# Release order kept, the last pair's weights by blocks in turn, row sums through TensorE, and a reordered start and routing end

## The chip, the cores and the metric

The kernel runs on one core of a Trainium2 chip. The metric is the device time of one execution in microseconds (us). Engines are named as the profile names them: PE is TensorE's matmul (PEld its weight load), DVE is VectorE, ACT is ScalarE, POOL is GpSimd, and SP is SyncE, whose queue issues most DMA transfers.

## The reference, cut to what matters

One encoder layer on 512 tokens of width 1024 in float32: an embedding layer norm, two attentions (A windowed with a sink, B latent) that read one projection `w_in`, their output projection, a layer norm, a mixture of 32 experts (each token goes to one group of 8 and to two experts in it), and a last layer norm.

```python
    h = layer_norm(x, ln_emb_g, ln_emb_b)
    proj = h @ w_in[l]
    ...
    h = layer_norm(DEEPNORM_ALPHA * h + mixed, ln_attn_g[l], ln_attn_b[l])
    ffn = hierarchical_moe(h, w_group[l], b_group[l], w_expert[l], b_expert[l], w_gate[l], w_up[l], w_down[l])
    h = layer_norm(DEEPNORM_ALPHA * h + ffn, ln_ffn_g[l], ln_ffn_b[l])
```

## The kernel before, in words

Tokens stand in four tiles of 128 (`xs[t]` as loaded, `z[t]` the residual stream), and the width of 1024 in two halves of 512. Products up to the routing are made in three passes on a split operand: `hth`/`htl` are the high and low part of the transposed, normed tokens, `wh`/`wl` those of a weight chunk `wf`. `split` makes the high part with a copy on ScalarE and the low part with a subtraction on another engine.

**The start.** The loop over `t` calls `layer_norm` (L203 and L204, two halves each: subtract the mean and multiply by the gain `lng`, then scale and add `lnb`), transposes the tile with the identity `ident`, which is a part of the constants `cst`, and splits the transposed values. The gain and the bias are loaded as 128 copies of a row, in four transfers on SP ahead of `cst`. For the first weight chunk POOL makes the low parts (L209). The first token tile's products begin with the high weights.

**The heads.** In two halves `c` of the heads, `heads` transposes and splits the queries of each token tile. Attention B's first units are scheduled beside the last of them.

**The routing's end.** The layer norm after attention is applied for tile 0, then 1, then `a` and `b` (tiles 2 and 3). `route(t)` picks a tile's experts in a chain of small DVE operations, `add_z` adds the output projection to `z`, `norm_gain`, `norm_bias`, `gain` and `shift` apply the norm, and `gather(t, ...)` collects the first two experts' tokens by products with a selection matrix into `gk`, which becomes `xT0`.

**The expert loop.** The experts are worked in 16 pairs. For a pair, `gates` (L1243) multiplies 64 gathered tokens of each of the two experts by `w_gu`, over 8 blocks `j` of the width, the two experts' products side by side in TensorE's columns; `gated` makes `hid`; `down` (L1263) multiplies by `w_dn`; `put` (L1276) weighs the result, adds the scaled residual of the gathered row, and `scatter` (L1269) writes the rows to `moe_rows` in HBM. Weights sit in a ring of six slots, and a pair's weights are asked for three pairs ahead, on SP, in `load_next` and `load_next_dn`: an issue waits until the products that read the old contents are done. In slots 0 and 1 the first half of `w_gu` is made of two pieces of 512 KB, so that they come free after two blocks each. Pair 0 runs two blocks of its gates, then the products `places` (L1368), which tell which rows the next pairs need, then the other six.

**The tail.** The last pair isn't scattered. `weighted` leaves its rows split in `y2`, and `pz_part` (L1310) multiplies them by `sT`, the transposed selection of their tokens, into `pz` in PSUM. The rows of the other pairs come back from `moe_rows` as `rows0` and `rows1`, two for each token. `rows_add` (L1480) adds the two, `total` (L1503) adds `pz` and sums the row, `square` (L1509) sums the squares, `factor` makes the reciprocal root, and `scale`, `gain`, `bias` or `gain_first` and `scale_bias` (L1529, L1534) end the norm. The order on every engine is the written one here.

## Time and profile before

| | |
|---|---|
| median of three runs | 594.92 us (592.09 to 598.53) |
| the profiled execution | 591.33 us, its span 589.5 us |
| granted TensorE clock, mean | 0.970 of full speed |
| PE busy | 523.4 us (89%) |
| DVE busy | 322.6 us (55%) |
| ACT busy | 222.1 us (38%) |
| POOL busy | 99.9 us (17%) |
| read from HBM | 133.14 MB |

The span runs from the first to the last instruction of the profiled execution. Busy shares are means over stages that differ: up to about 327 us the products of the attentions and their projections, then the 16 pairs, and from 545 us the last pair and the final norm.

### The profile page before, as it was taken

The numbers are of one execution on the slowest core, as the hardware profiler recorded it, in microseconds if no ns is written. First come the engines' busy times: TensorE is split into PE (matmuls) and PEld (weight loads), VectorE is DVE, ScalarE is ACT, GpSimd is POOL, SyncE is SP. The second block draws the span as 40 slices with busy tenths as digits, with TensorE's granted clock in tenths as the row PEclk, the third lists the DMA queues.
The fourth block names the chain that finished last, engine by engine and source line by source line (L and its number), as shares of the span: only waits on it lengthen the run. The fifth ranks groups of instructions, "written<-read, shape, count | busy, mean of one in ns | idle before, by whom it ended". The sixth has DMA issues, their size and how long they took to land. (4 is left out here: it accounts for less than half of the span.)

```text
span 589.5 us, 8004 instructions
## 1 busy us (share of the span) xinstructions
PE 523.4 (89%) x2756; PEld 331.8 (56%) x2757; DVE 322.6 (55%) x882; ACT 222.1 (38%) x477; POOL 99.9 (17%) x141
## 2 busy tenths in 40 slices
...
GB/s 279 280 290 81 102 43 0 59 81 42 85 16 58 1 1 212 289 367 39 66 258 259 280 391 410 420 415 415 411 417 400 421 418 391 412 420 416 264 267 142
DMA packets 46268, 141.76 MB, mean 240 GB/s; under 512 B 12380, under 2 KB 19420, under 8 KB 37009
## 3 DMA queue, kind: packets, MB, share of 16 engines
...
q10 hardware_dynamic: 1152, 2.10, 0.9%
...
HBM read 133.14 MB, written 16.25 MB: 253 GB/s over the span
## 5 line engine op out<-in xcount | busy, mean ns | idle before, releaser
L1243 PE MATMUL p_gu<-w_gu,xT 128*64 128x512 f32 x512 | 125.0, 613 | 15.0 <-DMA w_gu<-in_w_gu 14.1
L1243 PEld LDWEIGHTS p_gu<-w_gu,xT 128*64 128x64 f32 x512 | 39.6, 141 | 95.6 <-issue 70.0
L1247 ACT ACTIVATE hid<-p_gu 128x256 f32<-128x256 f32 x16 | 6.1, 384 | 176.0 <-PE p_gu L1243 163.9
L1248 DVE TENSOR_TENSOR hid<-hid,p_gu 128x256 f32<-128x256 f32 x16 | 6.7, 421 | 113.9 <-ACT hid L1247 113.8
L1263 PE MATMUL p_y<-w_dn,hidT 128*64 128x512 f32 x256 | 59.9, 611 | 1.0 <-issue 0.6
L1276 DVE SCALAR_TENSOR_TENSOR xg<-p_y,wsl,xg 128x512 f32<-128x512 f32 x30 | 22.5, 751 | 28.4 <-PE p_y L1263 26.5
L1263 PEld LDWEIGHTS p_y<-w_dn,hidT 128*64 128x64 f32 x256 | 17.5, 140 | 31.4 <-issue 29.3
L604 PE MATMUL ptr<-cst,pr 128*128 128x128 f32 x208 | 33.3, 278 | 1.9 <-ACT pr L562 1.4
L1034 POOL DMA_INDIRECT xg<-norm_rows,tok x16 | 16.5, 1032 | 104.5 <-PE p_y L1263 16.8
L1269 POOL DMA_INDIRECT moe_rows<-xg,idx x15 | 15.6, 1039 | 95.0 <-DVE xg L1276 69.6
L604 PEld LDWEIGHTS ptr<-cst,pr 128*128 128x128 f32 x208 | 24.9, 145 | 9.5 <-ACT pr L562 3.2
L577 ACT ACTIVATE pr<-pmm,bnm 128x512 f32<-128x512 f32 x32 | 22.0, 689 | 10.6 <-DVE bnm L574 9.7
L574 DVE TENSOR_REDUCE bnm<-pmm 128x1 f32<-128x512 f32 x32 | 21.9, 687 | 5.3 <-PE pmm L215 4.8
L215 PE MATMUL pmm<-wh,htl 128*128 128x512 f32 (+1 forms) x64 | 24.0, 374 | 0.0
L213 PE MATMUL pmm<-wh,hth 128*128 128x512 f32 (+1 forms) x64 | 23.8, 372 | 0.0
L214 PE MATMUL pmm<-wl,hth 128*128 128x512 f32 (+1 forms) x64 | 23.5, 368 | 0.0
L562 ACT ACTIVATE pr<-pr,rc 128x512 f32<-128x512 f32 (+2 forms) x32 | 20.6, 645 | 4.1 <-DVE rc L560 3.9
L590 DVE CUSTOM_DVE_ANT_0 sm<-pmm,mask,nsink 128x256 f32<-128x256 f32 (+1 forms) x32 | 17.4, 545 | 7.6 <-PE pmm L587 6.5
L215 PE MATMUL pwo<-wh,htl 128*128 128x512 f32 (+1 forms) x56 | 20.7, 370 | 0.0
L214 PE MATMUL pwo<-wl,hth 128*128 128x512 f32 (+1 forms) x56 | 20.5, 367 | 0.0
L213 PE MATMUL pwo<-wh,hth 128*128 128x512 f32 (+1 forms) x56 | 20.5, 367 | 0.0
L1232 ACT ACTIVATE xg<-xg,of 128x1024 f32<-128x1024 f32 x15 | 17.2, 1149 | 8.5 <-PE p_x L1228 7.8
...
## 6 DMA issues: line engine op xcount, KB each, us to landing
...
```

The costliest lines, as they stand in the source:

```text
L213: PE.matmul(ps, ah, bh, start=first, stop=False)
L214: PE.matmul(ps, ah, bl, start=False, stop=False)
L215: PE.matmul(ps, al, bh, start=False, stop=last)
L562: SC.mul(pr[:, :n], pr[:, :n], rc)
L574: V.tensor_reduce(nm, sp, AX.X, ALU.max, negate=True)
L577: exps_.append(SC.activation(pr[:, :S], sp, AF.Exp, bias=nm, accum_out=den).ins)
L590: V.tensor_tensor_reduce(sm[:, :nk], sp[:, :nk], mask[:, mo:mo + nk], 1.0, nsink[:, h:h + 1], ALU.add, ALU.min, nm)
L604: PE.transpose(pt[:, k * P:(k + 1) * P], pr[:, k * P:(k + 1) * P], ident)
L1232: SC.mul(pl["xg"], pl["xg"], pl["of"])
L1243: PE.matmul(pg[64 * i:64 * i + 64], xT[:, j, 64 * i:64 * i + 64], ws[i][0][j], start=(j == 0), stop=(j == 7))
L1263: r = PE.matmul(py[64 * i:64 * i + 64, :], hT[:, j, 64 * i:64 * i + 64], ws[i][1][n][:, j], start=(j == 0), stop=(j == 1))
L1276: V.scalar_tensor_tensor(y, py, pl["wsl"], y, ALU.mult, ALU.add)
```

## The change

- **Start.** `cst` and the gain and bias as columns (`geT`) are loaded first, on ACT's queue. ScalarE writes (x - mean) / deviation into `z`; gain and bias are applied to the transposed values, where they are one number to a partition, and `hf` holds the result in SBUF. The first chunk's low weights are made by DVE. The order of the first two token tiles is written by hand, and their products alternate. `z` itself gets gain and bias later, in 16 DVE operations of 128x512 after the `heads` of each tile, from `lgb`, which SP loads as 128 copies of a row when the second half of the heads begins.
- **Slots 0 and 1.** The half that consists of two pieces is the second half now.
- **Routing's end.** `norm_gain` and `norm_bias` of the second half of `a` come earlier; `route(a)` is cut after five steps and goes on behind `add_z(1)` and its statistics; `gather(a)` takes its second half first, and `shift(b, 1)` stands ahead of `gain(b, 0)`.
- **Pair 0.** Its blocks go in the order 4 to 7, 0 to 3. The four row fetches go in the order 1, 0, 2, 3, with `weights(1)` ahead of them. The work on the next pairs' columns and weights is moved behind `down`'s products, ahead of `put`.
- **Loads by blocks in turn.** Pair 3's and the last pair's `w_gu` are asked for block by block, one expert after the other, and the last pair's `w_dn` half by half.
- **Tail.** All `rows_add` are on DVE, the first tile's ahead of `weighted`'s `put`. `pz` starts with a product of the identity and the added rows. ScalarE takes the sum and the sum of squares of each half from PSUM, `gain_first` reads PSUM, and all four tiles end with `scale_bias`. The gain is multiplied by the root of 1024 ahead of time.

```diff
             return t
+        geT = cp.tile([P, 2, NK], F32, name="geT")
+        SC.dma_start(out=cst, in_=A["cst"][:, :C_KEEP])
+        SC.dma_start(out=geT, in_=A["ge_T"])
         load_x(0)
-        lg, lb = [lp.tile([P, D], F32, name=nm) for nm in ("lng", "lnb")]
-        for n in range(2):
-            for dst, nm in ((lg, "ln_emb_g"), (lb, "ln_emb_b")):
-                SY.dma_start(out=dst[:, 512 * n:512 * n + 512], in_=A[nm][512 * n:512 * n + 512].partition_broadcast(P))
-        SY.dma_start(out=cst, in_=A["cst"][:, :C_KEEP])
...
-                split(wf[:, :, :n], wh[:, :, :n], wl[:, :, :n], PO if nch[0] == 0 else V)
+                if nch[0]:
+                    split(wf[:, :, :n], wh[:, :, :n], wl[:, :, :n])
+                else:
+                    wfs.append(wf)
...
+        def scaled_x(t, kk):
+            rs, nb = nrm[t]
+            sl = slice(512 * kk, 512 * kk + 512)
+            SC.activation(z[t][:, sl], xs[t][:, sl], AF.Identity, scale=rs, bias=nb)
...
+                g_, b_ = [geT[:, i, 4 * kk + k:4 * kk + k + 1] for i in range(2)]
+                if eng is SC:
+                    SC.activation(hf[:, k], pt[:, k * P:(k + 1) * P], AF.Identity, scale=g_, bias=b_)
+                else:
+                    V.tensor_scalar(hf[:, k], pt[:, k * P:(k + 1) * P], g_, b_, ALU.mult, ALU.add)
...
+        with tc.manual_schedule(engines={V.engine, SC.engine, PE.engine, PO.engine}):
+            stats_half(0, 0)
+            stats_half(0, 1)
+            stats_end(0)
+            stats_shift(0)
             for kk in range(2):
-                pt = ptr()
-                for k in range(4):
-                    PE.transpose(pt[:, k * P:(k + 1) * P],
-                                 z[t][:, (4 * kk + k) * P:(4 * kk + k + 1) * P], ident)
-                pv = pt.rearrange("p (a b) -> p a b", a=4)
-                o = (slice(None), slice(4 * kk, 4 * kk + 4), slice(t * P, (t + 1) * P))
-                split(pv, hth[o], htl[o])
+                scaled_x(0, kk)
+                turn_x(0, kk)
+            gain_x(0, 0, range(4), V)
+            w_high(0)
+            stats_half(1, 0)
+            gain_x(0, 1, (1,), SC)
+            high(0, 0)
+            first_mm(0, hth, 0, 0)
+            low(0, 0)
...
-                heads(qt_, qth, qtl, c, t)
+                with tc.issue_after(heads(qt_, qth, qtl, c, t)):
+                    zt = z[t][:, 512 * c:512 * c + 512]
+                    V.tensor_tensor(zt, zt, lgb[0][:, c], ALU.mult)
+                    V.tensor_tensor(zt, zt, lgb[1][:, c], ALU.add)
...
-            if i == 0 and slot < 2:
-                return [(f"gu{slot}0{q}", 2 * q, 2) for q in range(2)]
+            if i == 1 and slot < 2:
+                return [(f"gu{slot}1{q}", 4 + 2 * q, 2) for q in range(2)]
...
+        def load_turns(e, slots, order):
+            ws = [{}, {}]
+            for h in order:
+                for ts in zip(*[gu_tiles(sl, h) for sl in slots]):
+                    for i in range(2):
+                        tag, j, n = ts[i]
+                        ws[i].update(zip(range(j, j + n), load_blocks(e + i, slots[i], tag, j, n)))
+            return [[w[j] for j in range(NK)] for w in ws]
...
-        place(a)
+        steps(ra)
+        place(1)
         sel0_(1)
-        sel0_(a)
         logits(b, 0)
         logits(b, 1)
         offset(b)
...
-        norm_gain(a, 1)
         biased(b)
-        norm_bias(a, 1)
         for i in range(2):
             keep(a, i)
         gather(0, range(2))
...
+        count(a)
         gather(1, range(2))
         steps(route(b))
+        place(a)
+        sel0_(a)
         count(b)
-        gather(a, [0])
         gain(b, 1, V)
+        gather(a, [1])
         place(b)
         sel0_(b)
-        gather(a, [1])
+        gather(a, [0])
+        shift(b, 1, V)
         gain(b, 0, V)
-        shift(b, 1, V)
...
+                pys.append(py)
+                if not between:
+                    put(slice(512 * n, 512 * n + 512), py)
+            if between:
+                between()
+                for n in range(2):
+                    put(slice(512 * n, 512 * n + 512), pys[n])
             return r.ins
...
+        def pz_rows(t, n, rows):
             tg = tags[t, n]
             pzs[t, n] = ps.tile([P, 512], F32, name="pz", tag=tg, bufs=1 if tg in ("psd", "pac") else 2)
+            PE.matmul(pzs[t, n], ident, rows, start=True, stop=False)
+        def pz_part(t, n, sT, y2):
             for k in range(2):
-                PE.matmul(pzs[t, n], sT[:, t * P:(t + 1) * P], y2[k][n], start=(k == 0), stop=(k == 1))
+                PE.matmul(pzs[t, n], sT[:, t * P:(t + 1) * P], y2[k][n], start=False, stop=(k == 1))
...
+                order = 4, 5, 6, 7, 0, 1, 2, 3
+                gates(pg, xT, ws[p], order, 0, 2)
+                first_rows()
+                gates(pg, xT, ws[p], order, 2)
             else:
-                gates(pg, xT, ws[p], 0, 8)
+                gates(pg, xT, ws[p])
...
-                pi = psd("places")
-                places_mm(pi, sels[1], [weights_of(2 + u) for u in range(2)], range(NT))
-                places_weights(pi, [plc[2], plc[3]], 6, 3, 1)
+                residual(0)
+                for u, sel in ((0, sel0), (2, sels[1])):
+                    pi = psd("places")
...
-            gates(pg, xT, ws[p], 0, 8)
+            gates(pg, xT, ws[p])
         hT = gated(pg)
-        y2 = [ring(slots(p)[0], f"gu0{k}", [P, D], F32R, "y2") for k in range(2)]
+        y2 = [ring(slots(p)[0], f"gu1{k}", [P, D], F32R, "y2") for k in range(2)]
         y2 = halves(y2)
+        for n in range(2):
+            rows_add(0, n, V)
         weighted(p, hT, y2)
-        for t in range(NT):
+        st = [[small.tile([P, n], F32, name=f"st{t}{i}", bufs=1) for i, n in enumerate((2, 1, 2, 1, 1))] for t in range(NT)]
+        def total(t):
+            for n in range(2):
+                pz_rows(t, n, half(rows0, t, n))
             for n in range(2):
...
-        st = [[small.tile([P, n], F32, name=f"st{t}{i}", bufs=1) for i, n in enumerate((2, 1, 1, 1, 1))] for t in range(NT)]
...
+        def square(t):
+            sm, nm, sq = st[t][:3]
             V.tensor_scalar(nm, sm[:, 0:1], sm[:, 1:2], -1.0 / D, ALU.add, ALU.mult)
-        def square(t):
-            sm, nm, sq, rs, nb = st[t]
-            jk = wk[0].tile([P, D], BF16, name="jk", tag="xT", bufs=3)
-            SC.activation(jk, rows0[t], AF.Square, bias=nm, accum_out=sq)
...
         def scale_bias(t):
-            rs = st[t][3]
+            sm, nm, sq, rs, var = st[t]
+            V.tensor_scalar(var, sq[:, 0:1], sq[:, 1:2], LN_EPS * D, ALU.add, ALU.add)
+            PO.tensor_tensor(rs, var, mhalf[:, :1], ALU.pow)
+            yield
             for n in range(2):
                 V.scalar_tensor_tensor(half(rows1, t, n), half(rows1, t, n), rs, half(gbs, 1, n), ALU.mult, ALU.add)
-                leave(t, n)
...
-        gbs = gb[:, 0], gb[:, 1]
-        for t in range(2):
-            for n in range(2):
-                rows_add(t, n, PO)
-        total(0)
+                rows_add(t, n, V)
         square(0)
+        gain_first(0)
         total(1)
-        square(1)
-        for n in range(2):
-            rows_add(2, n, V)
-        factor(0, True)
-        scale(0)
-        total(2)
-        square(2)
-        factor(1, True)
-        scale(1)
+        sb = [scale_bias(t) for t in range(NT)]
         for n in range(2):
             rows_add(3, n, V)
+        next(sb[0])
+        square(1)
+        gain_first(1)
+        steps(sb[0])
+        total(2)
+        next(sb[1])
+        square(2)
+        gain_first(2)
+        steps(sb[1])
         total(3)
+        next(sb[2])
         square(3)
-        gain(0)
-        bias(0)
-        gain(1)
-        factor(2, False)
-        bias(1)
-        gain_first(2)
-        factor(3, False)
-        scale_bias(2)
         gain_first(3)
-        scale_bias(3)
+        steps(sb[2])
+        next(sb[3])
+        steps(sb[3])
```

The first of the places, DVE where the last queries are split and attention B begins: `bnm` is the maximum of a row of scores, `qtl` the low part of the queries. Before:

```order
L209 TENSOR_TENSOR qtl<-ptr,qth 96x4x128 [waits Activation_49]
L574 TENSOR_REDUCE bnm<-pmm 128x1 [waits PE_49]
L323 SCALAR_TENSOR_TENSOR rp_1615<-pwo,rq_337,ctb 128x128 [waits Activation_49]
L331 SCALAR_TENSOR_TENSOR rp_1616<-pwo,rq_337,stb 128x4x16 [waits DVE_49]
L331 SCALAR_TENSOR_TENSOR rp_1616<-pwo,rq_337,stb 128x4x16
L209 TENSOR_TENSOR qtl<-ptr,qth 96x4x128 [waits Activation_49]
```

After:

```order
L584 TENSOR_TENSOR qtl<-ptr,qth 96x4x128 [waits Activation_49]
L619 TENSOR_TENSOR z_64<-z_64,ln_emb_g 128x512
L695 TENSOR_REDUCE bnm<-pmm 128x1 [waits PE_49]
L441 SCALAR_TENSOR_TENSOR rp_1676<-pwo,rq_426,ctb 128x128 [waits Activation_49]
L449 SCALAR_TENSOR_TENSOR rp_1677<-pwo,rq_426,stb 128x4x16 [waits DVE_49]
L449 SCALAR_TENSOR_TENSOR rp_1677<-pwo,rq_426,stb 128x4x16
L584 TENSOR_TENSOR qtl<-ptr,qth 96x4x128 [waits Activation_49]
L619 TENSOR_TENSOR z_65<-z_65,ln_emb_g 128x512
L620 TENSOR_TENSOR z_64<-z_64,ln_emb_b 128x512 [waits DVE_49]
```

Between the split of the queries and `bnm` now stands one of the operations that bring gain or bias into `z`, and two more follow after the next split.

The second place, SP's queue at the loads of pair 3, which are asked for in pair 0. Before (`w_gu` of 128x1024 is a piece of 512 KB, of 128x2048 one of 1 MB):

```order
L692 DMA w_gu_3971<-in_w_gu 128x1024 [waits DMAHW7_49,PE_49]
L692 DMA w_gu_3973<-in_w_gu 128x1024 [waits DMAHW0_49,PE_49]
L692 DMA w_gu_3975<-in_w_gu 128x2048 [waits DMAHW1_49,PE_49]
L692 DMA w_gu_3977<-in_w_gu 128x1024 [waits DMAHW2_49]
L692 DMA w_gu_3979<-in_w_gu 128x1024 [waits DMAHW3_49]
L692 DMA w_gu_3981<-in_w_gu 128x2048 [waits DMAHW4_49,PE_49]
L709 DMA w_dn_4020<-in_w_dn 128x1024 [waits DMAHW5_49,PE_49]
L709 DMA w_dn_4021<-in_w_dn 128x1024 [waits DMAHW6_49,PE_49]
```

After:

```order
L817 DMA w_gu_4038<-in_w_gu 128x1024 [waits DMAHW6_49,PE_49]
L817 DMA w_gu_4040<-in_w_gu 128x1024 [waits DMAHW7_49,PE_49]
L817 DMA w_gu_4042<-in_w_gu 128x1024 [waits DMAHW0_49,PE_49]
L817 DMA w_gu_4044<-in_w_gu 128x1024 [waits DMAHW1_49,PE_49]
L817 DMA w_gu_4046<-in_w_gu 128x2048 [waits DMAHW2_49,PE_49]
L817 DMA w_gu_4048<-in_w_gu 128x2048 [waits DMAHW3_49,PE_49]
L843 DMA w_dn_4113<-in_w_dn 128x1024 [waits DMAHW4_49,PE_49]
L843 DMA w_dn_4114<-in_w_dn 128x1024 [waits DMAHW5_49,PE_49]
```

Before, the second expert's pieces of 512 KB stand behind the first expert's 1 MB; now the four pieces of 512 KB stand ahead of both.

The third place, DVE at the end of the last pair. Before:

```order
L1248 TENSOR_TENSOR hid<-hid,p_gu 128x256 [waits Activation_49]
L1254 COPY hidT<-p_t 128x256 [waits DVE_49,PE_49]
L1331 SCALAR_TENSOR_TENSOR xg<-p_y,wsl,xg 128x512 [waits DMASW2_49,PE_49]
L209 TENSOR_TENSOR y_5496<-xg,y_5495 128x512 [waits DMAHW4_49,DMAHW2_49,DMAHW6_49,DMAHW0_49,Activation_49]
L1331 SCALAR_TENSOR_TENSOR xg<-p_y,wsl,xg 128x512 [waits PE_49]
L209 TENSOR_TENSOR y_5496<-xg,y_5495 128x512 [waits Activation_49]
L1503 ISA rows_5458,st_5537<-pz,rows_5458 128x512 [waits DMAHW3_49,DMAHW1_49,DMAHW5_49,DMASW7_49,DMAHW7_49,PE_49,Pool_49]
L1503 ISA st_5537 128x1
L1503 ISA rows_5458,st_5537<-pz,rows_5458 128x512 [waits PE_49,Pool_49]
L1503 ISA st_5537 128x1
```

After:

```order
L1395 TENSOR_TENSOR hid<-hid,p_gu 128x256 [waits Activation_49]
L1401 COPY hidT<-p_t 128x256 [waits DVE_49,PE_49]
L1650 TENSOR_TENSOR rows_5526<-rows_5526,rows_5528 128x512 [waits DMAHW3_49,DMAHW4_49,DMAHW2_49,DMAHW6_49,DMAHW0_49,DMASW7_49]
L1650 TENSOR_TENSOR rows_5526<-rows_5526,rows_5528 128x512
L1488 SCALAR_TENSOR_TENSOR xg<-p_y,wsl,xg 128x512 [waits DMASW2_49,PE_49]
L205 TENSOR_TENSOR y_5564<-xg,y_5563 128x512 [waits DMAHW4_49,Activation_49]
L1488 SCALAR_TENSOR_TENSOR xg<-p_y,wsl,xg 128x512 [waits PE_49]
L205 TENSOR_TENSOR y_5564<-xg,y_5563 128x512 [waits Activation_49]
L1650 TENSOR_TENSOR rows_5526<-rows_5526,rows_5528 128x512 [waits DMAHW5_49,DMAHW4_49]
L1650 TENSOR_TENSOR rows_5526<-rows_5526,rows_5528 128x512
L1650 TENSOR_TENSOR rows_5527<-rows_5527,rows_5529 128x512 [waits DMAHW6_49,DMAHW7_49,DMAHW1_49,DMASW0_49]
L1650 TENSOR_TENSOR rows_5527<-rows_5527,rows_5529 128x512
```

Tile 0's row additions, which POOL made, stand ahead of the two weighings of the last pair's rows, and those of tiles 1 and 2 right behind them.

## Rows read from the trace of the kernel before

**Rows 1.** Windows of stages: window and its us, then each engine's busy us, PEclk, DMA share, GB/s

```profile
30.00:105.00 75.00, 75.00 (x409) 64.37 (x408) 39.64 (x109) 36.61 (x78) 10.68 (x19) 1.00 0.31 99
...
346.00:545.00 199.00, 180.41 (x855) 70.14 (x856) 62.57 (x174) 29.86 (x44) 28.53 (x27) 0.97 1.01 412
...
545.00:590.00 45.00, 21.85 (x82) 8.76 (x78) 25.23 (x53) 10.07 (x16) 11.16 (x11) 0.79 0.57 222
```

**Rows 2.** Timeline of the embedding norm: start, us, engine, line, operation, idle before and its releaser

```profile
8.01 0.75 DVE L203 SCALAR_TENSOR_TENSOR z<-xt,ln_mv,lng 128x512 f32<-128x512 f32 x1 [2.32 <-DMA lng<-in_ln_emb_g]
...
10.53 1.95 PE L257 MATMUL ptr<-cst,z 128*128 128x128 f32 x8 [10.53 <-DMA cst<-cst]
...
13.23 1.22 PE L385 MATMUL pwo<-wh,hth 128*128 128x512 f32 x2 [0.76 <-ACT wh L208]
...
16.57 8.05 POOL L209 TENSOR_TENSOR wl<-wf,wh 128x1024 fp32r<-128x1024 f32 x3
...
16.77 5.61 DVE L204 SCALAR_TENSOR_TENSOR z<-z,ln_rs,lnb 128x512 f32<-128x512 f32 x2
...
19.75 1.09 PE L257 MATMUL ptr<-cst,z 128*128 128x128 f32 x4 [2.10 <-DVE z L204]
```

**Rows 3.** Windows around the start of attention B

```profile
132.00:153.00 21.00, 20.97 (x126) 20.40 (x125) 10.73 (x29) 8.21 (x16) 3.52 (x6) 1.00 0.13 36
...
156.00:159.00 3.00, 2.54 (x11) 1.94 (x12) 3.00 (x10) 1.52 (x5) 0.91 (x2) 0.80 0.41 102
...
159.00:162.00 3.00, 3.00 (x14) 2.51 (x13) 2.29 (x7) 2.16 (x7) 0.00 (x0) 0.63 0.33 132
```

**Rows 4.** Timeline of the routing's end and pair 0

```profile
312.20 0.14 DVE L850 TENSOR_REDUCE gm<-lgt 128x1 f32<-128x4 f32 x1
...
314.59 0.74 DVE L1098 SCALAR_TENSOR_TENSOR z<-pwo,rr,z 128x512 f32<-128x512 f32 x1
...
326.92 1.94 PE L1243 MATMUL p_gu<-w_gu,xT 128*64 128x512 f32 x8 [0.78 <-DVE gn L892]
...
328.88 9.21 SPq L692 DMA_DIRECT2D w_gu<-in_w_gu  x6
```

**Rows 5.** Windows of pair 0

```profile
330.00:336.00 6.00, 6.00 (x31) 2.28 (x30) 4.62 (x31) 0.00 (x0) 1.86 (x2) 1.00 0.68 208
...
336.00:339.00 3.00, 1.24 (x12) 1.21 (x10) 1.97 (x8) 1.53 (x2) 2.39 (x3) 0.95 0.64 193
...
339.00:342.00 3.00, 3.00 (x9) 1.12 (x11) 0.48 (x3) 0.00 (x0) 0.01 (x1) 0.50 1.00 385
```

**Rows 6.** Timeline of the last pair and the tail

```profile
554.12 0.20 PEld L1243 LDWEIGHTS p_gu<-w_gu,xT 128*64 128x64 f32 x4 [0.97 <-DMA w_gu<-in_w_gu]
...
557.89 4.60 SPq L1484 DMA_DIRECT2D rows<-moe_rows  x8
...
559.79 3.65 PE L1263 MATMUL p_y<-w_dn,hidT 128*64 128x512 f32 x16 [0.56 <-issue]
...
563.13 2.95 POOL L1480 TENSOR_TENSOR rows<-rows,rows 128x512 f32<-128x512 f32 x2 [12.28 <-DMA rows<-moe_rows]
...
567.04 4.84 PE L1310 MATMUL pz<-y,sT 128*128 128x512 f32 x13 [0.23 <-DVE y L209]
...
568.71 1.15 ACT L1509 ACTIVATE jk<-rows,st 128x1024 bf16<-128x1024 f32 x1 [2.44 <-DVE st L1504]
...
570.34 1.29 DVE L1480 TENSOR_TENSOR rows<-rows,rows 128x512 f32<-128x512 f32 x2
...
582.24 0.99 POOL L183 TENSOR_TENSOR st<-rsq_t,mhalf 128x1 f32<-128x1 f32 x1 [1.06 <-DVE rsq_t L181]
...
584.73 1.41 DVE L1534 SCALAR_TENSOR_TENSOR rows<-rows,st,gb 128x512 f32<-128x512 f32 x2
```

**Rows 7.** Line L405 by form: ns min/median/max, first and last start

```profile
L405 ACT ACTIVATE junk<-pwo x2: 597/597/597, 30.1 to 39.8; 128x512 bf16<-128x512 f32 x2
...
L405 ACT ACTIVATION_READ_ACCUMULATOR junk<-pwo x2: 194/196/197, 30.6 to 40.3; 128x1 f32 x2
```

270 lines of the change are left out of this document (179 added, 91 removed).

## The prediction

> **What bounds the kernel now.** I read the windows by stage first, then the timeline inside the stages that the change touches, then the windows again wherever it moves a load. From 30 to 105 us PE has work in all 75.00 us, and over the 16-pair loop the DMA share is 1.01 while PE works 180.41 of 199 us; in the last 45 us PE works 21.85 and DVE 25.23 [rows 1]. So there are three regimes: up to the routing a microsecond saved in front of PE moves all that follows; in the pair loop the weight stream is the clock, and only a gap in it can be won; behind the last weights a chain through DVE sets the end. The sum below is made against the profiled execution, 591.33 us. The median of the three runs is 594.92, so 3.59 us go on top at the end, and differences are carried over unchanged.
>
> **Part 1, the start.** In the trace DVE waits 2.32 us for the gain's load before the first operation of the norm at 8.01, the first transpose starts at 10.53 after a wait for `cst`, and the first product at 13.23 [rows 2]. With `cst` first on another queue and no broadcast loads, nothing but the statistics is left ahead of ScalarE's scaling. The 2.32 us go from in front of 8.01, and with the root of the variance ScalarE can begin at about 6.3; from there I count 0.8 for a half on ScalarE, 1.1 for four transposes (1.09 [rows 2]), 1.2 for four gain operations, 0.6 for a high copy and 0.3 for hand-offs: an estimate of 10.3 for the first product. A second loss follows: the low parts on POOL take 8.05 us for three from 16.57, and DVE's two additions of the bias beside them take 5.61 us, and the second tile's transposes wait for these, until 19.75 [rows 2]. In the changed order POOL has no such work, but the second tile's statistics stand on DVE behind the gains and a low part, and `w_low(0)` to `w_low(3)`, 128x1024 each, some 1.3 us at two halves of 0.64 [rows 6], come on top. I put the point from which PE runs without a gap at 16.6 instead of 19.75, three microseconds earlier, with about as many products done by then. As PE is full from there to 105 us, the gain is carried in full: **-3.0 us**. The bounds: -5 if the second tile isn't late at all (the 2.9 us at the first product and the 2.1 us that PE idles ahead of 19.75 [rows 2] both go), -1 if the 1 MB pieces of the first chunk, whose turn comes after the same 1 MB of tokens, hold PE at the third quarter.
>
> **Part 2, gain and bias for `z`.** They are 16 operations of 128x512 on DVE at 0.64 us each (two in 1.29, of that shape [rows 6]), 10.3 us in all. The first eight fall where DVE is busy 10.73 of 21 us [rows 3], so its idle time hides them. The loads from `lgb` are 1 MB on a queue with a DMA share of 0.13 there [rows 3], and cost nothing. The last eight, 5.2 us, stand ahead of attention B's row maxima. DVE is full in 156 to 159 and at 2.29 of 3 in the next window, and PE, which lacks work for 0.46 us in the first, has already fallen to a granted clock of 0.63 in the second [rows 3]. There nothing hides them; a backlog of 5.2 us is worked off at about 0.7 us of DVE idle time in 3 us, and PE runs ahead meanwhile with the other units' scores. I take **+1.5 us**, from 0 (the scheduler's other work fills PE) to +3.5 (the backlog less what two windows take up, 1.4).
>
> **Part 3, routing and pair 0.** On DVE `add_z(1)` at 314.59 follows the chain of `route(a)`, which starts at 312.20 with operations of 0.14 us and more, and the first gates come at 326.92 [rows 4]. Cutting `route(a)` after five of its dozen steps lets `add_z` go some 1.3 us earlier; two operations of 0.75 us (as that of 314.59) on tile `a` leave the path ahead of `route(b)`; and only blocks 4 to 7 are needed for the first gates, so these begin some 2.8 us earlier. None of that is a gain by itself, since the next regime is the weight stream's. What counts is its gap: from 330 to 339 the DMA share is 0.68 for 6 us and 0.64 for 3 us, and 1.00 from 339 on [rows 5], so 1.9 + 1.1 = 3.0 us of the stream are lost. SP's six issues for pair 3 lie from 328.88 over 9.21 us [rows 4]: the first two pieces are let go by the first two blocks, the third, 1 MB, by the eighth, and the second expert's small pieces, which were free, queue behind it. In the new order four small pieces are asked for ahead of the large ones, 2 MB instead of 1 MB before the last gates end, and everything is asked for 2.8 us earlier against a stream that itself ran dry when its queue was empty. Moving `columns` and the weights behind `down` takes DVE's work away from in front of `hid`. I take **-2.2 us** of the 3.0; -0.5 if only the shift of the gates counts, in part; -3.5 if the half clock at 339 to 342 [rows 5] goes as well. The price would be paid in `between`: `put` of pair 0 now waits on DVE behind two places' weights, about 2 us, but pair 1's gates don't wait for it.
>
> **Part 4, the last pair's loads in turn.** The second group of gates waits 0.97 us for its piece at 554.12 [rows 6]. By turns the gates can end 1.4 us earlier. The row loads hide this: they start at 557.89, take 4.60 us, and the first additions start at 563.13 [rows 6]; in the changed order `put` stands behind these additions on DVE. Zero, and what is late next is the rows.
>
> **Part 5, the tail.** Before, `y2` is complete when the last products begin at 567.04 [rows 6]. Now DVE does the two additions first (1.29), then two `put`s of 0.75 with a high copy and a low part each in turn, so `y2` comes at 568.7. From 563.13 DVE's list is: additions 8 x 0.64 = 5.1, `put` and low parts 2.9, with 1.4 of waiting for the copies, `gain_first` and `scale_bias` 16 x 0.70 (1.41 for two [rows 6]) = 11.2, twelve small ones of 0.14 (as at 312.20 [rows 4]) 1.6, the last root on POOL 1.0 (0.99 [rows 6]): 23.2, hence 586.3. The end before is 584.73 + 1.41 = 586.14 [rows 6]. That list has no wait for ScalarE. A half of a sum costs it 0.60 + 0.19 us [rows 7], of a square, with a pointer, about 0.72 + 0.19 (1.15 for a whole row of 1024 [rows 6], less half a row); four tiles take 13.6 us, each square waiting for a mean on DVE. Followed instruction by instruction that chain ends at 588.3, without overlap on ScalarE. I take the middle, **+1.2 us**. The identity products are hidden at full clock: two `w_dn` products side by side need 3.65 / 4 = 0.91 us (sixteen records, two to a product [rows 6]), which I take for one of full width; with the four products of `y2` a tile needs 2.7 us on PE, and DVE needs 4.3. The bounds are -0.9 (one wait for a copy and a faster root) and +5.7 (the first rival).
>
> **The sum.** -3.0 + 1.5 - 2.2 + 1.2 = -2.5 us: 588.8 for the profiled execution, 592.4 for the median.
>
> **Rival 1, slower: the identity products at half clock.** In 339 to 342, after PE had idled, the granted clock was 0.50, 1.2 GHz [rows 5], and the thirteen products from 567.04 take 4.84 us [rows 6], 0.37 each. PE waits for DVE between the last pair's `w_dn` and `y2`, so it can come to the tail at 1.2 GHz and, with gaps between tiles, stay there. A tile then needs 2 x 1.83 + 4 x 0.5 = 5.7 us on PE; the last three end at 569.9 + 17 = 587, and sum, mean, squares, root and two operations follow until 591.8: +5.7 in the tail, +2.0 in all, 596.9. It decides once a tile's PE time exceeds DVE's 4.3. Against it: PE's work per tile is larger than before, and thirteen products in 4.84 us are quicker than at half clock throughout, 13 x 0.5. The Trainium skill (TensorE: Matmul & The Clock Gate, Part 1: The HAM clock gate) says that an idle array is slowed to half its clock and that activity gives the full clock back; the trace agrees on the fall (0.50), and whether it comes back in this tail no run here shows. Chance 0.15; with a start that gains 1 and a pair 0 that gains 0.5 this rival passes 601.
>
> **Rival 2, faster by over 1%: all covers hold.** The start gains 5, pair 0 gains 3.0, the `z` work is hidden, the tail is even: -8.0, 586.9. For it speaks that both starting losses are waits that the change removes, and that the stream's gap is plainly visible; against it that DVE takes over POOL's work. Chance 0.29.
>
> **Rival 3: the stream's gap stays.** If the gap is set by how long pair 0's eight gates take rather than by the order of the pieces, part 3 gives -0.5 and the sum is -0.8: 594.1. Chance 0.17. The forecast has the remaining 0.39.
>
> **Chances and range.** About 1%, 5.9 us, is what a measurement of this kernel can tell from no change. Faster takes most of rival 2 and a fifth of the forecast's spread: 0.35. Slower takes the upper part of rival 1 and of the bounds of parts 2 and 5: 0.10. The rest, 0.55, is within 1%. The range reaches from just below rival 2 to just above rival 1: 585.5 to 597.5.
>
> **What would show it.** Right: first product near 10.3 and PE without gaps from 16.6; the windows behind the first gates of pair 0 at a DMA share near 1; the last scores of tile 0 in attention B late by one to two us; the last operation some 2.5 us earlier than 584.73. Wrong: a PE idle window at the first chunk's later quarters, a share near 0.65 again behind pair 0's gates, or identity products of 1.8 us with DVE idle between tiles.

## The result and the profile after

The changed kernel takes 599.89 us (median of 19 runs, 594.45 to 603.92); the kernel before took 594.13 in 19 runs beside it. The ratio is 1.0079 (95% interval 1.0055 to 1.0103), about 4.7 us slower; the two medians lie 5.8 apart. The forecast, 592.4 with a range up to 597.5, was wrong. The profiled execution of the changed kernel took 596.65 us, span 595.0, mean granted clock 0.966; it is 3.2 us quicker than the median, so what one profile shows need not hold for all executions.

**The start** is quicker, as forecast. Its timeline (start, us, engine, line, operation, idle before and releaser):

```profile
10.97 1.22 PE L309 MATMUL pwo<-wh,hth 128*128 128x512 f32 x2 [1.25 <-ACT hth L292]
...
17.30 1.36 PE L276 MATMUL ptr<-cst,z 128*128 128x128 f32 x8 [0.85 <-ACT z L271]
```

The first product stands at 10.97 instead of 13.23, and the second tile's transposes wait 0.85 us instead of 2.10 [rows 2]. How far this lasts is read from a copy that both kernels make at the same place of the first projection (`cqt`, L396 before): its last one starts at 70.6 before and at 67.4 after. The views of the line, before and after:

```profile
L396 ACT COPY cqt<-pmm x4: 580/586/588, 33.9 to 70.6; 128x512 f32<-128x512 f32 x4
L507 ACT COPY cqt<-pmm x4: 577/592/632, 32.6 to 67.4; 128x512 f32<-128x512 f32 x4
```

**The start of attention B** takes it away. Windows of the changed kernel (columns as in [rows 1]):

```profile
151.00:154.00 3.00, 0.74 (x6) 0.49 (x5) 2.90 (x7) 2.17 (x6) 0.26 (x2) 1.00 0.70 233
154.00:157.00 3.00, 2.52 (x9) 1.49 (x10) 3.00 (x9) 0.58 (x1) 1.64 (x2) 0.66 0.00 0
157.00:160.00 3.00, 3.00 (x11) 2.25 (x10) 3.00 (x7) 1.48 (x4) 0.30 (x1) 0.50 0.57 175
160.00:163.00 3.00, 2.61 (x12) 1.99 (x10) 3.00 (x7) 1.93 (x5) 0.00 (x0) 0.70 0.00 0
```

DVE is busy in 11.90 of the twelve microseconds. PE works 0.74 of the first three, and then runs at 0.66, 0.50 and 0.70 of its clock. The timeline shows who waits and what DVE does meanwhile:

```profile
151.71 0.68 DVE L619 TENSOR_TENSOR z<-z,ln_emb_g 128x512 f32<-128x512 f32 x1
152.31 0.68 DVE L695 TENSOR_REDUCE bnm<-pmm 128x1 f32<-128x512 f32 x1
...
153.85 0.50 PE L209 MATMUL pmm<-kth,qth 96*128 96x512 f32 x1 [2.26 <-ACT pr L698]
...
156.91 0.68 DVE L695 TENSOR_REDUCE bnm<-pmm 128x1 f32<-128x512 f32 x1
```

PE waits 2.26 us for `pr`, which ScalarE makes from the row maximum `bnm`, and `bnm` stands behind an operation on `z`. But most of that wait isn't new. The same place in the kernel before:

```profile
154.88 0.68 DVE L574 TENSOR_REDUCE bnm<-pmm 128x1 f32<-128x512 f32 x1
...
156.47 0.50 PE L213 MATMUL pmm<-kth,qth 96*128 96x512 f32 x1 [1.71 <-ACT pr L577]
...
157.46 0.69 DVE L574 TENSOR_REDUCE bnm<-pmm 128x1 f32<-128x512 f32 x1
```

There PE waited 1.71 us, from 154.76 to 156.47, and ran at 0.63 in 159 to 162 [rows 3]; the windows of [rows 3] begin at 156 and show only the end of that wait. The work on `z` adds 0.55 us to it, and then it holds up the next row maxima: from the first to the second it takes 4.60 us instead of 2.58, from the first to the fourth 9.26 (152.31 to 161.57) instead of 6.49 (154.88 to 161.37).

**Pair 0.** Windows of the changed kernel, the first two those of [rows 5]:

```profile
330.00:336.00 6.00, 5.76 (x29) 2.01 (x28) 5.11 (x37) 2.67 (x12) 0.60 (x1) 1.00 1.01 414
336.00:339.00 3.00, 1.09 (x6) 0.54 (x8) 1.62 (x6) 0.22 (x1) 2.39 (x3) 1.00 0.94 350
...
350.00:354.00 4.00, 4.00 (x22) 1.29 (x18) 0.90 (x3) 0.00 (x0) 1.10 (x1) 1.00 0.69 215
```

The gap of the weight stream at 330 to 339 is closed: the shares are 1.01 and 0.94 instead of 0.68 and 0.64. But a new gap stands at 350 to 354, with a share of 0.69, where the kernel before had 0.98:

```profile
350.00:354.00 4.00, 3.65 (x20) 1.18 (x16) 0.42 (x1) 0.69 (x2) 0.00 (x0) 1.00 0.98 379
```

The timeline of the changed kernel, for this execution:

```profile
314.97 0.80 SPq L817 DMA_DIRECT2D w_gu<-in_w_gu  x2
...
326.42 1.94 PE L1390 MATMUL p_gu<-w_gu,xT 128*64 128x512 f32 x8
...
335.40 1.26 POOL L1178 DMA_INDIRECT xg<-norm_rows,tok  x1 [17.88 <-DVE cmb L1056]
...
338.34 5.35 PE L1411 MATMUL p_y<-w_dn,hidT 128*64 128x512 f32 x16 [0.51 <-DVE hidT L1401]
...
344.41 1.06 PE L1374 MATMUL p_x<-cst,xg 128*128 128x128 f32 x8 [0.71 <-DMA xg<-norm_rows,tok]
...
346.52 1.05 PE L1140 MATMUL psd<-cmb,sel 128*128 128x6 f32 x8 [0.26 <-DVE pis L1165]
...
347.50 7.09 PE L1390 MATMUL p_gu<-w_gu,xT 128*64 128x512 f32 x32
...
351.18 0.33 SPq L817 DMA_DIRECT2D w_gu<-in_w_gu  x1
```

And the same stretch of the kernel before:

```profile
335.41 1.01 POOL L1034 DMA_INDIRECT xg<-norm_rows,tok  x1 [0.31 <-DVE wc L910]
...
339.13 5.11 PE L1263 MATMUL p_y<-w_dn,hidT 128*64 128x512 f32 x16
...
344.17 1.09 PE L1228 MATMUL p_x<-cst,xg 128*128 128x128 f32 x8
...
345.98 4.51 PE L1243 MATMUL p_gu<-w_gu,xT 128*64 128x512 f32 x20
349.66 0.33 SPq L692 DMA_DIRECT2D w_gu<-in_w_gu  x1
```

Pair 0's gates begin 0.50 us earlier than before (326.92 [rows 4]) and its `down` ends 0.55 earlier (343.69 against 339.13 + 5.11 = 344.24). Yet pair 1's gates begin 1.52 later, at 347.50 instead of 345.98. Counted from the mark, SP's issue at 314.97 above and at 313.26 in the kernel before (it waits for the end of the output projection), pair 0's gates begin 2.21 us earlier (11.45 instead of 13.66) and pair 1's only 0.19 (32.53 instead of 32.72), so that what pair 0's gates won is lost in between. Three things stand there: `p_x`, the transposes of the fetched rows, waits 0.71 us for these rows, a second `places` product of 1.03 stands on PE ahead of the gates, and it waits 0.26 for a copy on DVE. Pair 1's gates release the slots for pair 4, so SP's next issue also comes 1.52 late, and the stream runs dry there instead. Pair 1's rows were fetched at the same time as before (335.40 against 335.41), but the fetch took 8.9 us from issue to landing, before 6.9: it now shares the DMA engines with a weight stream that has no gap.

Not every execution of this pair 0 has the new gap. In the profiles of three kernels below with the same pair 0 ("old tail", "last pair by expert", "earlier") `p_x` waits for nothing and pair 1's gates begin 31.11 to 31.14 us behind the mark. In "earlier" pair 1's rows land after 5.2 us, and the stream's share is 0.91 or more in each window from 327 to 358. In these three the six later blocks of pair 0's gates took 7.07 us instead of 5.37, at a granted clock near 0.6.

**The tail**, timeline of the changed kernel:

```profile
553.09 0.97 POOL L1423 DMA_INDIRECT moe_rows<-xg,idx  x1 [16.75 <-DVEq L1613]
...
566.52 1.29 DVE L1650 TENSOR_TENSOR rows<-rows,rows 128x512 f32<-128x512 f32 x2 [6.18 <-DMA rows<-moe_rows]
...
567.27 3.11 PE L1463 MATMUL pz<-rows,cst 128*128 128x512 f32 x4 [3.17 <-DVE rows L1650]
...
571.24 0.69 DVE L205 TENSOR_TENSOR y<-xg,y 128x512 fp32r<-128x512 f32 x1 [0.69 <-ACT y L204]
...
582.04 0.69 ACT L1685 ACTIVATE jk<-pz,st 128x512 bf16<-128x512 f32 x1 [1.23 <-DVE st L1683]
...
585.87 0.69 ACT L1685 ACTIVATE jk<-pz,st 128x512 bf16<-128x512 f32 x1 [1.23 <-DVE st L1683]
...
590.21 1.41 DVE L1698 SCALAR_TENSOR_TENSOR rows<-rows,st,gb 128x512 f32<-128x512 f32 x2 [0.66 <-POOL st L1695]
```

The first row addition comes at 566.52, 3.39 us later than before (563.13 [rows 6]); the scatter of pair 14, on which these rows wait, left at 553.09 instead of 549.88. From there to the end of the last operation it takes 25.10 us, 23.01 before: the tail itself is 2.1 longer. Four profiles with this tail agree: from that scatter to the end of the last operation they take 38.5 to 38.6 us, five with the old tail 35.6 to 37.4. `y2` is complete at 571.93, 5.4 us behind the landed rows instead of 3.9 [rows 6]. Then the tiles follow each other through ScalarE in 3.83 us each (582.04 to 585.87), of which it waits 1.23 for the mean on DVE. Two windows show the clock under the identity products:

```profile
568.00:571.00 3.00, 3.00 (x5) 1.09 (x4) 1.83 (x3) 1.03 (x2) 0.00 (x0) 0.50 1.03 408
571.00:580.00 9.00, 8.71 (x25) 4.56 (x25) 7.07 (x14) 5.98 (x18) 0.57 (x1) 0.98 0.25 101
```

### The profile page after: what moved, and what is told of

It is laid out like the page before. It is cut to its first block, busy times and chain, and to the rows that moved or that the text cites. A ratio compares the mean times of both kernels' runs of the same rounds, so it can differ in the third digit from the quotient of the medians.

```text
span 595.0 us, 8067 instructions
## 1 busy us (share of the span) xinstructions
PE 535.5 (90%) x2772; PEld 333.0 (56%) x2773; DVE 325.7 (55%) x898; ACT 236.7 (40%) x518; POOL 82.7 (14%) x131
## 4 chain that ended last, share of the span: by engine, by line
PE 46%; DMA 33%; DVE 12%; ACT 4%; issue 3%; SPq 1%; POOL 1%; POOLq 0%; DVEq 0%; ACTq 0%
DMA w_gu<-in_w_gu 27%; PE p_gu L1390 5%; PE pwo L210 5%; PE pwo L211 5%; PE pwo L209 5%; PE pmm L209 4%; PE pmm L210 4%; PE pmm L211 4%; PE ptr L725 3%; PE pac L759 3%; PE pac L1190 2%; DMA xg<-norm_rows,tok 1%; DMA rows<-moe_rows 1%; DMA xt<-in_x 1%; DMA moe_rows<-xg,idx 1%
## 5 line engine op out<-in xcount | busy, mean ns | idle before, releaser
L1390 PE MATMUL p_gu<-w_gu,xT 128*64 128x512 f32 x512 | 126.5, 625 | 11.8 <-DMA w_gu<-in_w_gu 11.7
L211 PE MATMUL pmm<-wh,htl 128*128 128x512 f32 (+1 forms) x56 | 20.8, 372 | 0.0
L210 PE MATMUL pmm<-wl,hth 128*128 128x512 f32 (+1 forms) x56 | 20.5, 367 | 0.0
L1374 PEld LDWEIGHTS p_x<-cst,xg 128*128 128x128 f32 x120 | 13.3, 140 | 12.9 <-issue 8.1
L209 PE MATMUL pmm<-wh,hth 128*128 128x512 f32 (+1 forms) x56 | 20.4, 364 | 0.0
```

The lines of the kernel that those rows point to most:

```text
L209: PE.matmul(ps, ah, bh, start=first, stop=False)
L210: PE.matmul(ps, ah, bl, start=False, stop=False)
L211: PE.matmul(ps, al, bh, start=False, stop=last)
L1390: PE.matmul(pg[64 * i:64 * i + 64], xT[:, j, 64 * i:64 * i + 64], ws[i][0][j], start=(n == 0), stop=(n == NK - 1))
```

## Experiments

The first number is the median in us, the second the ratio on record to runs of the kernel before beside it, with a 95% interval; twelve runs each unless said. The ratio isn't the quotient of the two medians (the kernel before had 593.28, 594.81 and 594.19 in the three series) and differs from it by up to 0.3%. Differences in us go by the ratios. Most intervals reach 0.3% to each side, 1.8 us.

**Without the work on `z`.** The 16 operations are gone, so that the residual stream lacks gain and bias.

```diff
-                with tc.issue_after(heads(qt_, qth, qtl, c, t)):
-                    zt = z[t][:, 512 * c:512 * c + 512]
-                    V.tensor_tensor(zt, zt, lgb[0][:, c], ALU.mult)
-                    V.tensor_tensor(zt, zt, lgb[1][:, c], ALU.add)
+                heads(qt_, qth, qtl, c, t)
```

> The changed kernel without the 16 operations that bring gain and bias into z after the heads; the residual lacks them, so its values are others. Theory M (these operations, on a full DVE at the start of attention B, cost about 4.9 us there, through waits of PE and the half clock that follows, and the loss is carried to the end): 4 to 5 us less than the changed kernel, ratio to the kernel before 0.999 to 1.002; PE's idle time and the low clock at 151 to 163 as before the change or less. Rival W (the weight stream absorbs what is lost ahead of it): at most 1.5 us less, ratio 1.005 or more.

Measured: 592.98, 0.9974 (0.9946 to 1.0002), 1.05% or some 6 us below the changed kernel. Its window at the place:

```profile
151.00:163.00 12.00, 10.64 (x57) 7.32 (x59) 10.39 (x29) 8.99 (x23) 0.92 (x2) 1.00 0.23 73
```

PE works 10.64 us at the full clock, against 8.87 (the sum of the four windows above) at a lower one. PE's first wait is as in the kernel before, 1.71 us, and here no fall of the clock follows:

```profile
151.90 0.50 PE L209 MATMUL pmm<-kth,qth 96*128 96x512 f32 x1 [1.71 <-ACT pr L694]
```

From the first row maximum to the fourth it takes 6.01 us (150.32 to 156.33), against 9.26. The operations cost more than DVE's 5.2 us of backlog.

**The same work on GpSimd.**

```diff
-                    V.tensor_tensor(zt, zt, lgb[0][:, c], ALU.mult)
-                    V.tensor_tensor(zt, zt, lgb[1][:, c], ALU.add)
+                    PO.tensor_tensor(zt, zt, lgb[0][:, c], ALU.mult)
+                    PO.tensor_tensor(zt, zt, lgb[1][:, c], ALU.add)
```

> The changed kernel with the 16 operations on GpSimd in place of VectorE, nothing left out. Theory M: DVE's list at the start of attention B is as short as without them, so nearly all of that run's gain, ratio 1.000 to 1.003. Rival P (GpSimd and VectorE get in each other's way as in the first stage of the kernel before, 2.8 us an operation): no gain, ratio 1.006 or more, with DVE operations of two SBUF inputs stretched beside GpSimd's.

Measured (six runs): 605.01, 1.0192 (1.0144 to 1.0240). Theory M missed; the ratio is in the range of rival P. Timeline of POOL, and of DVE beside it:

```profile
108.93 10.00 POOL L619 TENSOR_TENSOR z<-z,ln_emb_g 128x512 f32<-128x512 f32 x8 [1.59 <-DMA ln_emb_g<-in_ln_emb_g]
...
124.41 0.61 POOL L594 COPY ktok<-krr 128x128 f32<-128x128 f32 x1
...
120.12 5.41 DVE L478 SCALAR_TENSOR_TENSOR w2l<-wf,gq,w2h 128x384 fp32r<-128x384 f32 x4 [3.88 <-ACT w2h L477]
```

The idle GpSimd took all of the work at once, from 109 us, at 1.25 us (10.00 / 8) for each of the products with the gain, and a copy of the keys (`ktok`), for which PE waits, stood behind it: in 120 to 125 us PE does nothing. Rival P's sign is there too: four operations of DVE with two SBUF inputs take 5.41 us beside it, where in the changed kernel each takes 0.61. What PE waits for longest is the copy (5.6 us), so the order on the new engine was the larger cost; that DVE's stretched operations cost nothing isn't shown. The run says nothing on the second place, the start of attention B.

**The same work earlier, on DVE.** Half 0 goes behind the heads of the second half of the keys, half 1 behind the first half of the queries, and `lgb` is loaded one stage earlier. `z_whole` holds the two operations.

```diff
-                heads(kt_, kth, ktl, c, t)
+                mark = heads(kt_, kth, ktl, c, t)
+                if c == 1:
+                    with tc.issue_after(mark):
+                        z_whole(t, 0)
...
+                mark = heads(qt_, qth, qtl, c, t)
+                if c == 0:
+                    with tc.issue_after(mark):
+                        z_whole(t, 1)
```

> The changed kernel with all its work, but the 16 operations on z earlier: one half behind the second half of the keys' heads, the other behind the first half of the queries' heads, with their loads at the start of the keys' heads. Theory M (it is the place, a full DVE at the start of attention B, that costs, not the work): the first row maximum and the end some 4 to 6 us earlier than in the changed kernel, ratio to the kernel before 0.997 to 1.000, near the run without the operations. Rival D (DVE's idle time in the heads is not free, since PE waits for the low parts of keys and queries that now queue behind these operations): 2 us or less gained, ratio 1.004 or more.

Measured: 595.45, 1.0022 (0.9991 to 1.0053), 0.57% or 3.4 us below the changed kernel. The profiles can be compared at the mark, SP's issue of two weight pieces ahead of pair 0. A profile is one execution: this kernel's took 589.15 us, 6.3 less than its median. The mark in each, with the granted clock of two stretches:

| profile | work on `z` | mark, us | clock 151 to 157 | clock 180 to 190 |
|---|---|---|---|---|
| this one | earlier | 309.50 | 1.00 | 1.00 |
| start alone (below) | earlier | 310.14 | 0.81 | 1.00 |
| old pair 0 (below) | earlier | 310.69 | 0.78 | 1.00 |
| earlier, old tail (below) | earlier | 313.22 | 0.72 | 0.66 |
| no between (below) | earlier | 313.37 | 0.72 | 0.66 |
| fetch first (below) | earlier | 312.80 | 1.00 | 0.66 |
| pair 3 in turn (below) | earlier | 313.40 | 0.72 | 0.66 |
| additions behind (below) | earlier | 309.92 | 0.75 | 1.00 |
| without | none | 311.26 | 1.00 | 0.72 |
| the change | in place | 314.97 | 0.83 | 1.00 |
| old tail (below) | in place | 318.14 | 0.95 | 1.00 |
| last pair by expert (below) | in place | 317.82 | 0.93 | 1.00 |

Kernels with the same work up to the mark come there some 3 us apart; with the work earlier, it is the clock in 180 to 190 us by which they part. Single profiles can't settle less than that. Between profiles that kept the clock there, the place of the change costs 4.3 to 8.6 us: 314.97 to 318.14 against 309.50 to 310.69. Between those that lost it, the earlier place costs at most some 2 us: 312.80 to 313.40 against 311.26 without the work, at 0.66 and 0.72.

**The old tail.** The changed kernel with the tail of before.

```diff
-        for n in range(2):
-            rows_add(0, n, V)
         weighted(p, hT, y2)
-            PE.matmul(pzs[t, n], ident, rows, start=True, stop=False)
...
-                SC.activation(junk(), pzs[t, n], AF.Identity, accum_out=sm[:, n:n + 1])
+                V.tensor_tensor_reduce(half(rows0, t, n), pzs[t, n], half(rows0, t, n), 1.0, 0.0, ALU.add, ALU.add, sm[:, n:n + 1])
```

> The changed kernel with the tail of the kernel before (additions of the first two tiles on GpSimd, sums on VectorE, no identity products, gain not scaled ahead). Theory T (the new tail is a ring through ScalarE of 3.83 us a tile and starts with additions ahead of the last pair's weighing, 2.1 us longer from the rows' landing on): 2 us less than the changed kernel, ratio 1.004. Rival R (the end is set by when the rows land, and the two tails are worth the same from there): within 0.6 us of the changed kernel, ratio 1.007 to 1.009.

Measured: 595.10, 1.0036 (1.0006 to 1.0065), 0.43% or 2.6 us below the changed kernel; the intervals overlap, and the profiles' 2.1 agrees.

**The last pair's loads expert by expert.**

```diff
-                if p == 0 or p + 3 == NP - 1:
+                if p == 0:
...
-                dns = load_dns(e, sl) if p + 3 == NP - 1 else [load_dn(e + i, sl[i]) for i in range(2)]
+                dns = [load_dn(e + i, sl[i]) for i in range(2)]
```

> The changed kernel with the last pair's weights asked for expert by expert as before; pair 3 stays in turn. Theory L (the pieces in turn let the last pair's bytes in beside pair 14's, so pair 14's second weights land 3 us later and its rows with them): 2 to 3 us less, ratio 1.003 to 1.005, and pair 14's scatter issues 2 to 3 us earlier against its gates of pair 13. Rival S (the whole stream is late by the shift of its start, whatever the order of the last pieces): within 0.6 us, ratio 1.007 to 1.009.

Measured (six runs): 599.07, 1.0102 (1.0059 to 1.0146). The last pair's loads in turn gave nothing that these runs can tell.

**The work on `z` earlier and the old tail.** The two edits above together.

```diff
+                        z_whole(t, 0)
...
-        for n in range(2):
-            rows_add(0, n, V)
```

> As the run before this one, and with the tail of the kernel before. If the two losses add, 2.5 us less than that run, ratio 0.993 to 0.996, faster than the kernel before; if the weight stream takes back what the start wins, 0.998 or more.

Measured: 594.28, 0.9994 (0.9968 to 1.0020). The first expectation missed: with both known costs gone the start's gain should have been left, and it wasn't; the old tail is worth 0.28%, 1.7 us, between these two kernels. The ratio is that of the second expectation, that the weight stream takes the gain back. Either it does so in general, or a third cost stood between the start and the tail; the next two kernels tell.

**The start alone.** The kernel before with the new start and the work on `z` in the earlier place.

```diff
-        lg, lb = [lp.tile([P, D], F32, name=nm) for nm in ("lng", "lnb")]
+        geT = cp.tile([P, 2, NK], F32, name="geT")
+        SC.dma_start(out=cst, in_=A["cst"][:, :C_KEEP])
...
+                        z_whole(t, 0)
```

> The kernel before with the new start alone, the 16 operations on z early as in the two runs before; routing, pair 0, loads and tail as before. Theory F (the 3 us won in front reach the end through PE and through earlier weight loads): 3 us less than before, ratio 0.994 to 0.996. Rival W (the weight stream alone sets the end of the pairs, and its loads wait for slots that the start doesn't free earlier): ratio 0.999 to 1.001.

Measured: 590.46, 0.9933 (0.9905 to 0.9960). The start is worth 4.0 us when its work on `z` is hidden, and the weight stream doesn't take that back.

**The old pair 0.** The same plus the new end of the routing, and nothing else of the change; against the kernel of "earlier and the old tail" it takes back pair 0, the pieces and the loads in turn of pair 3 and of the last pair.

```diff
-                order = 4, 5, 6, 7, 0, 1, 2, 3
-                gates(pg, xT, ws[p], order, 0, 2)
-                first_rows()
-                gates(pg, xT, ws[p], order, 2)
+                gates(pg, xT, ws[p], 0, 2)
...
-            last = run_pair(p, xT, meanwhile, None if p else between)
+            last = run_pair(p, xT, meanwhile)
```

> The run with early z and the old tail, with pair 0, the loads of pair 3 and of the last pair also as before; start and the routing's end stay changed. Theory G (pair 0's new order closes the stream's gap of 3 us behind its gates but opens another of 1.5 us or more at 350 to 358, since pair 1's rows are fetched no earlier): within 1.5 us of that run, ratio 0.993 to 0.997, with a DMA share near 0.65 behind pair 0's gates and near 1 at pair 1. Rival H (the gap closed in pair 0 is worth its 2 to 3 us at the end): 2 to 3 us more than that run.

Measured: 590.09, 0.9934 (0.9902 to 0.9965), as quick as the start alone. So the end of the routing is worth nothing that these runs can tell, and pair 0 with its loads doesn't give, it costs, 0.60% or 3.6 us (the two intervals leave 1 to 6). Rival H is out. Of theory G the ratio and the shares came, but the two kernels aren't within 1.5 us. In the timeline of this kernel `p_x` has no wait:

```profile
340.48 1.09 PE L1358 MATMUL p_x<-cst,xg 128*128 128x128 f32 x8
...
342.29 4.08 PE L1373 MATMUL p_gu<-w_gu,xT 128*64 128x512 f32 x18
```

From the start of pair 0's `down` (335.23) to pair 1's gates it takes 7.06 us, 6.85 before, 9.16 in the changed kernel and 9.93 in the kernel of "earlier and the old tail". That last one and the kernel before pass the mark together, 313.22 and 313.26, so that their stream can be compared. Here its window, then that of the kernel before:

```profile
300.00:358.00 58.00, 52.74 (x318) 33.58 (x318) 35.38 (x142) 12.99 (x27) 7.01 (x8) 0.94 0.78 287
```

```profile
300.00:358.00 58.00, 52.75 (x328) 34.06 (x329) 37.15 (x153) 13.37 (x28) 7.20 (x8) 0.97 0.79 295
```

Although its pair 0 began 2.26 us earlier (324.66 against 326.92), it had moved 8 GB/s x 58 us = 464 KB less by 358 us, about 1.1 us of the stream, and pair 14's scatter left at 551.20 instead of 549.88.

The times show the 3.6 us; the profiles alone wouldn't. From the mark to pair 14's scatter it takes 234.94 us here, 236.62 in the kernel before and 239.28 in "start alone", all with the old pair 0. With the new one it takes 238.12 in the changed kernel, 237.98 in "earlier and the old tail", 236.01 to 237.23 in four others and 241.98 in the kernel with the additions behind (below). A part lies behind pair 1's gates: from their start to that scatter the three old ones take 203.3 to 204.7 us, these seven 204.7 to 206.1.

**Parts of pair 0.** Three kernels cut it further, and a fourth asks where the tail's loss comes from. First, the old place of the side work, in the kernel of "earlier and the old tail":

```diff
                 if p == 0:
+                    if i == 0:
+                        residual(0)
+                    else:
+                        pi = psd("places")
+                        places_mm(pi, sel0, [weights_of(u) for u in range(2)], range(NT))
...
-            last = run_pair(p, xT, meanwhile, None if p else between)
+            last = run_pair(p, xT, meanwhile)
```

> The run with early z and the old tail, in which pair 0's side work goes back to where it was (the residual and the first weights' products ahead of down, the columns and the second weights behind its put); the block order, the rows' fetches and the loads stay new. Theory Q (pair 1's gates stand in PE's queue behind two products for weights where it was one, and so the loads that they release come late): pair 1's gates start about 6.9 us behind pair 0's down instead of 9.9, or 8.4 where the rows' fetch is what is left; the share of the DMA engines at pair 1 rises, ratio 0.995 to 0.998. Rival L (the loads in turn let the ring run dry whatever PE does): as without the edit, 0.998 to 1.001.

Second, in that one, `weights(1)` behind the fetches again:

```diff
-            weights(1)
...
-            for t in range(2, NT):
+            for t in range(1, NT):
                 weights(t)
```

> As the run before this one, and tile 1's weights computed behind the rows' fetches as before the change, so that the first fetch doesn't queue behind eight operations of DVE. Theory Q: the first fetch issues 0.9 us earlier against pair 0's gates, pair 1's gates by as much, ratio 0.993 to 0.996, as with the old pair 0. Rival: rows land no earlier, since their packets queue behind the weights; ratio as in the run before this one.

Third, the kernel with the old pair 0, with pair 3's loads in turn:

```diff
+                if p == 0:
+                    ws[p + 3] = [(gu, None) for gu in load_turns(e, (s0, s1), (0, 1))]
+                else:
```

> The run with early z, old tail and old pair 0, with one part of the new pair 0 alone: pair 3's weights are asked for block by block, the small pieces of both experts first. Theory G (four small pieces ahead of the large ones close part of the stream's gap behind pair 0's gates, and nothing else moves): the DMA share there rises from about 0.7 to 0.8 or more, ratio 0.990 to 0.993. Rival N (the stream is short of released slots, so what goes early leaves the gap later): 0.993 to 0.996.

Fourth, in the kernel with the work on `z` earlier, the first tile's row additions behind the last pair's weighings:

```diff
+        weighted(p, hT, y2)
         for n in range(2):
             rows_add(0, n, V)
-        weighted(p, hT, y2)
```

> The run with early z and the new tail, with tile 0's additions behind the weighing of the last pair's rows. Theory T: the last pair's split rows are complete about as long before the rows' landing as the additions take, so the tail from the landing of the rows to the last operation is 1.3 us shorter; the rest of its 2.1 us stays with the ring through ScalarE; ratio 0.2 percent under that run's, 0.998 to 1.001. Rival: the ring of 3.8 us a tile alone sets the tail, and its length from the landing of the rows doesn't change.

Measured: 593.07 and 0.9949 (0.9912 to 0.9987), 591.38 and 0.9967 (0.9942 to 0.9992), 592.51 and 0.9961 (0.9923 to 1.0000), 593.08 and 0.9951 (0.9912 to 0.9989). The first three lie between the kernels that they were to tell apart, and no two of the four are apart by more than their intervals. Their profiles say more than their times.

- With the old place of the side work only one `places` product stands ahead of pair 1's gates, yet from `down` to these gates it still takes 9.12 us, where theory Q had 6.9 to 8.4 and its base took 9.93. ScalarE waited for pair 0's rows until 344.71, so that `xT` came late and the gates waited 1.96 us for it. The second product is not what held them.
- With `weights(1)` behind the fetches the first fetch left 9.00 us behind pair 0's gates, without that edit 8.74: no earlier, and the theory's 0.9 us are out. `weights(1)` doesn't hold the fetch. The last of the rows that the fetch reads were written to HBM (`norm_rows`) from 323.1, 10.1 us ahead of it; in the changed kernel it was 10.1 us too (325.3 to 335.40). So the landing of these writes is the likely releaser; no run tests it.
- Pair 3's loads in turn alone, in the kernel with the old pair 0, show in their profile what the whole new pair 0 shows. Windows some 20 us behind the mark, first of the kernel with the old pair 0, then of this one, and what follows in this one:

```profile
330.00:333.00 3.00, 2.10 (x10) 0.43 (x6) 2.65 (x15) 0.39 (x1) 1.98 (x2) 1.00 0.56 168
```

```profile
333.00:336.00 3.00, 1.81 (x10) 0.36 (x6) 2.65 (x15) 0.38 (x1) 2.13 (x2) 1.00 0.99 363
...
344.63 1.09 PE L1369 MATMUL p_x<-cst,xg 128*128 128x128 f32 x8 [1.26 <-DMA xg<-norm_rows,tok]
...
350.00:354.00 4.00, 4.00 (x22) 1.36 (x18) 0.00 (x0) 0.38 (x1) 0.00 (x0) 1.00 0.88 282
```

The share rises from 0.56 to 0.99. Pair 1's rows land 9.4 us after their issue instead of 7.7, `p_x` waits 1.26 us for them where it waited for nothing, and the share falls later, to 0.88 in 350 to 354. From pair 1's gates to pair 14's scatter it takes 204.95 us instead of 203.34. That is what rival N said, what goes early leaves the gap later, and the ratio lies just above its range; theory G's "nothing else moves" is out. How the 3.6 us divide between the side work, the fetches' place and the loads in turn stays open by the times.
- The additions behind the weighings show their place: from pair 14's scatter to the end of the last operation it takes 37.24 us (551.90 to 589.14), 38.53 in the changed kernel and 36.26 before, so the additions ahead of the weighings are 1.3 of the tail's loss. By the ratio this kernel lies 0.7% below its base, by the median 2.4 us, more than these 1.3 us can be; why stays open. Its pair 0 also shows the new wait at its largest:

```profile
341.01 1.27 PE L1381 MATMUL p_x<-cst,xg 128*128 128x128 f32 x8 [4.12 <-DMA xg<-norm_rows,tok]
```

Here `down` of pair 0 began early, at 333.24, and 4.12 us of that PE waited away for the rows that pair 1 needs.

## Why the prediction was wrong

**Part 1, the start, -3.0: right, a little small.** PE is 3.2 us ahead at the `cqt` copy, and alone the start is worth 4.0. The first product came at 10.97 for an estimated 10.3. PE isn't without gaps from 16.6 on (it waits 0.85 us ahead of 17.30 and 0.41 ahead of 24.22), but they are short.

**Part 2, `z`, +1.5: the mechanism was right, the size too small.** It measured 3.4 by the median of the earlier placement, 4.9 at the mark, and 6 when left out; the bound of +3.5 was too low, and by its own terms (5.2 less 1.4) it is 3.8. The term counted DVE's backlog and let PE run ahead with other scores. PE couldn't: the fourth row maximum came 9.26 us behind the first instead of 6.49, and PE ran at 0.66, 0.50 and 0.70 meanwhile. The prediction also misread the kernel before: PE didn't fall to 0.63 after lacking work for 0.46 us but after waiting 1.71, most of which lies ahead of its window. That wait and a low clock behind it were there already, so the change can't be charged with them.

**Part 3, routing and pair 0, -2.2: this step failed.** By the times it measured +3.6 (1 to 6). Two links of it held: the gates came earlier (behind the mark by 11.45 us instead of 13.66), and the gap at 330 to 339 closed. The link that broke is that a closed gap is won time and "pair 1's gates don't wait for it". They don't wait for `put`, but they wait for pair 1's rows, and the fetch of these goes over the same DMA engines: without the gap it lands 8.9 us after its issue instead of 6.9, and with the loads in turn alone 9.4 instead of 7.7. So pair 1's gates, which release the next slots, win almost nothing of it (0.19 us behind the mark), and the stream's gap moves to 350. The rival "the stream's gap stays" gave this no loss. That the delay is there, and that it comes with the loads in turn alone, single profiles show; that it is all of the 3.6 is not shown. Three profiles with the same pair 0 don't have it, some 1 us is lost behind pair 1's gates, and how the rest divides stays open.

**Part 4, the last pair's loads, 0: right.** Pair 15's gates ran without a stall and the rows were late next; taking the loads back changed nothing.

**Part 5, the tail, +1.2: right in kind.** It measured 2.1 in the profile and 1.7 to 2.6 by the ratios. The two estimates that the prediction took the middle of were DVE's list (0.2 late) and ScalarE's chain (2.2 late); the chain was the answer. `y2` came 5.4 us after the rows, estimated 5.6.

**The rivals.** The identity products fell to half clock only for the first tile: 3.11 us for its pairs, 0.50 in 568 to 571, then 0.98 on average to 580. Two products took 1.88 to 1.98 us there and PE idled little; ScalarE and DVE set the pace. By the rule that the prediction cited from the Trainium skill (TensorE: Matmul & The Clock Gate, Part 1: The HAM clock gate), activity gives the clock back, and here the trace agrees. The prediction's line that this rival passes 601 with a weak start and a weak pair 0 comes to 600.6 by its own terms.

**The sum.** By the ratios the parts are -4.0 for the start, +3.4 for the work on `z`, +3.6 for pair 0 and its loads and +1.7 to +2.6 for the tail, 4.7 to 5.6 us together; measured were 4.7. With +1.7 the sum is no check: these are the steps of one chain of kernels from the changed one to the one before, and they add up to 4.7 by construction. Only the 2.6 comes from another kernel. The error of 7.2 us against the forecast of -2.5 is for the most part that of part 3 (5.8), then part 2 (1.9), and part 1 took 1.0 back.
